# Weight sums of the MLP built from HBM to HBM during the mixers, and the first product's combinations on GpSimd

## The chip, the cores and the metric

The kernel runs on one core of one Trainium2 chip, in one launch. The metric is the device time of an execution in microseconds (us). In the profile PE is TensorE, PEld its weight loads, DVE is VectorE, ACT ScalarE, POOL GpSimd, and SP the engine that only issues DMAs.

## The reference

One decoder layer on 1024 tokens of width 1024, after 16 meta tokens, in fp32: an RMS norm and one input projection, three mixers (GLA, a gated linear attention with 4 heads; SWA, a sliding-window attention with 16 query heads; SSD, a Mamba-2 scan in 4 groups), their gated sum through an output projection, then the MLP that the change is about, and a last RMS norm.

```python
def _layer(x, ...):
    h = _rmsnorm(x, norm_mix)
    g_q, g_k, g_v, g_r, g_lr, s_q, s_k, s_v, m_z, m_xbc, m_dt, gate_logits = split(h @ w_in)
    y_a = _gla(...) @ w_branch_gla
    y_b = _swa(...) @ w_branch_swa
    y_c = _ssd(...) @ w_branch_ssd
    merged = gates[:, :, 0] * y_a + gates[:, :, 1] * y_b + gates[:, :, 2] * y_c
    x = x + (merged @ w_out) * vmask
    h2 = _rmsnorm(x, norm_mlp)
    x = x + (square(relu(h2 @ w_mlp_in)) @ w_mlp_out) * vmask     # 1024 -> 4096 -> 1024
    return x                                                       # then a last _rmsnorm
```

## The kernel before

**Products.** Every fp32 operand of a product is split into a rounded part (`hi`, type fp32r) and the rest (`lo`), and a product is three matmuls: hi times hi, hi times lo, lo times hi. ACT casts the `hi`, DVE subtracts for the `lo`. Weights come from HBM in tiles `w_raw` of 128x1024 (three buffers), whose halves go to `w_hi` and `w_lo`.

**Stages in their order:** norm and transposes (0 to 90 us), GLA (to 550), SWA (to 860), SSD (to 1580), the three branch products with their gates (to 1950), the output projection (to 2041), a transition in which the normed tokens `h2` are transposed and their combinations are formed and split (2041 to 2083), the first MLP product (to 2387), the second (2377 to 2737) and the last norm, written out at 2747.

**GLA** handles a head in 8 pairs of chunks. Each pair ends with a root on GpSimd (`rstd_of`, L88, named `grs`), DVE's scaling `og` and, after every fourth pair, transposes on TensorE. **SWA** has 32 blocks, in each of which GpSimd scales the weights `pe` (L540). **SSD** has 4 groups of 8 chunks. A chunk loads `ab` (512 KB, the sums of one group broadcast to all partitions, two buffers, L642), DVE and ACT make the decay matrix from it, TensorE multiplies it (L654), and GpSimd computes `y` (L662), `xe` (L669), the state `S` (L673) and the root `yrs` (L88).

**The MLP** is computed by Strassen-Winograd: both factors are taken as 2x2 blocks, and 7 products of blocks take the place of 8. The weight sums are s1 = a21+a22, s2 = s1+a11, s3 = a11+a21, s4 = s2+a12.
- The *first product* has 16 units of 256 columns (`w_unit`, `unit_a` to `unit_e`). Per unit: two loads of 512 KB, four sums on DVE (L922 to L925), seven splits (L933, L934), seven products of 12 matmuls with 512 columns. The outputs x11, x21, x22 of 128x512 and the negatives n12, n21 (ACT, L953) go to HBM. Only `unit_a` and `unit_b` of unit 0 (the products x11*a11 and x21*a12) stand in the transition.
- The *second product* has 4 quarters `q` of seven products of 48 matmuls (L1148 to L1151). Its operands are made by chains (`Chain`): SP loads the first summand, and GpSimd issues DMAs that add the next onto the tile in SBUF (L1105, `accum_op=add`, 512 KB each, 64 in all). A chain's tile is cast by L1124 (from the first product's outputs) or L1137 (weights), added to and cast again.

**What sets the order:** the framework orders each engine's instructions and each queue's DMAs when the program is built; on the chip every engine works through its list in order, waiting where a semaphore says so. DMAs of SP and ACT go through hardware queues, those of GpSimd through a software queue.

Of the kernel before, what the change touches and what calls it, by code (L numbers as in the profile page):

```python
# [8 lines left out]
F32 = mybir.dt.float32  # L9
# [7 lines left out]
P = 128  # L17
# [27 lines left out]
def hybrid_layer_kernel(ctx, tc, x, meta_tokens, norm_mix, w_in, b_gate, gla_w_gate_up, gla_b_gate_up,  # L45
# [37 lines left out]

    def rstd_of(ss, n, name, rows=P, cols=1):
# [3 lines left out]
        nc.gpsimd.tensor_tensor(rs[:rows, :cols], ms[:rows, :cols], mhalf[:rows, :cols], ALU.pow)  # L88
        return rs[:rows, :cols]
# [12 lines left out]
    def vec(nm, i):  # L102
# [11 lines left out]
             for q in range(8) for n in ("x11", "x21", "x22", "n12", "n21")}  # L114
# [4 lines left out]
    def w_split(loads, cols, scales=None):  # L119
        hi = wp.tile([P, 2048], F32R, tag="whi", name="w_hi")  # L120
        lo = wp.tile([P, 2048], F32R, tag="wlo", name="w_lo")
        h = cols // 2
        for i in range(2):
            raw = raw_tile()
            loads(raw[:, :h], i)
            c = slice(i * h, (i + 1) * h)
            if scales is None:
                nc.scalar.copy(hi[:, c], raw[:, :h])  # L128
                nc.vector.tensor_tensor(lo[:, c], raw[:, :h], hi[:, c].bitcast(F32), sub)  # L129
                continue  # L130
            n = cols // len(scales)
            for k in range(h // n):
                sc, rc, c = scales[i * (h // n) + k], slice(k * n, (k + 1) * n), slice(i * h + k * n, i * h + (k + 1) * n)
                nc.scalar.activation(hi[:, c], raw[:, rc], AF.Copy, scale=sc)
                nc.vector.scalar_tensor_tensor(out=lo[:, c], in0=raw[:, rc], scalar=sc, in1=hi[:, c].bitcast(F32),
                                               op0=mult, op1=sub)
        return hi, lo

    def w_cols(view, ranges, scales=None):
        tot = sum(n for _, n in ranges)  # L140

        def loads(raw, i):
            rv = raw.rearrange("p (k c) -> p k c", k=KD // 2)
            o = 0
            for c, n in ranges:
                nc.sync.dma_start(rv[:, :, o:o + n], view[:, i * (KD // 2):(i + 1) * (KD // 2), c:c + n])
                o += n
        hi, lo = w_split(loads, KD * tot, scales)
        return (hi[:, :KD * tot].rearrange("p (k c) -> p k c", k=KD),
                lo[:, :KD * tot].rearrange("p (k c) -> p k c", k=KD))  # L150
# [16 lines left out]
    with p1:  # L167
# [118 lines left out]
        def gla():  # L286
# [15 lines left out]
            for h in range(4):  # L302
# [95 lines left out]
                for p in range(8):  # L398
# [23 lines left out]
                    rs = rstd_of(ss, 256, "grs")  # L422
                    nc.vector.scalar_tensor_tensor(out=og, in0=o, scalar=rs, in1=rt[p], op0=mult, op1=mult)
# [87 lines left out]
        def swa_block(sp, bk, sinks, m0, m1, kh, kl, vv, vvm, qq, h0, b):  # L511
# [28 lines left out]
            nc.gpsimd.tensor_tensor(pe[:, :, :nk], pe[:, :, :nk], up(zs, 2, [P, 4, nk]), mult)  # L540
# [17 lines left out]
        def ssd(g):  # L558
# [79 lines left out]
            with tc.high_priority(offset=HPE):  # L638
                for c in range(NT):
# [39 lines left out]
                    rs = rstd_of(ss, CH, "yrs")  # L679
                    nc.scalar.activation(y, y, AF.Copy, scale=rs)  # L680
# [6 lines left out]
        with tc.tile_pool(name="dtp", bufs=1, reuse_waits="tile") as dp, bank_pool("bdt") as bk:  # L687
# [6 lines left out]
            hi, lo = w_split(loads, KD * 64)  # L694
            w = (hi[:, :KD * 64].rearrange("p (k c) -> p k c", k=KD), lo[:, :KD * 64].rearrange("p (k c) -> p k c", k=KD))
# [73 lines left out]
    with ExitStack() as p2:  # L769
# [140 lines left out]

        def w_unit(u):
            raws = []
            for i in range(2):
                raw = raw_tile().rearrange("p (k c) -> p k c", k=4)
                nc.sync.dma_start(raw, wmi_v[:, 4 * i:4 * i + 4, u * 256:(u + 1) * 256])
                raws.append(raw)
            k4 = "p (k c) -> p k c"
            a11, a21 = raws[0][:, :, 0:P], raws[0][:, :, P:2 * P]
            a12, a22 = raws[1][:, :, 0:P], raws[1][:, :, P:2 * P]
            s1, s3 = (v.rearrange(k4, k=4) for v in m_tile())  # L920
            s2, s4 = (v.rearrange(k4, k=4) for v in m_tile())
# [5 lines left out]
            for names in (((1, a11), (6, s2), (5, s1), (2, a12)), ((7, s3), (4, a22), (3, s4))):  # L927
                hi = wp.tile([P, 2048], F32R, tag="whi", name="w_hi")
                lo = wp.tile([P, 2048], F32R, tag="wlo", name="w_lo")
                for i, (n, src) in enumerate(names):  # L930
                    h = hi[:, i * 512:(i + 1) * 512].rearrange(k4, k=4)
                    l = lo[:, i * 512:(i + 1) * 512].rearrange(k4, k=4)
                    nc.scalar.copy(h, src)  # L933
                    nc.vector.tensor_tensor(l, src, h.bitcast(F32), sub)  # L934
                    out[n] = (h, l)
# [15 lines left out]
        def neg(g):  # L951
            n = g_tile()
            nc.scalar.activation(n, g, AF.Copy, scale=-1.0)  # L953
            return n

# [277 lines left out]
```

## Time and profile before

| | us |
|---|---|
| three runs | 2742.92, 2743.89, 2758.51 (median 2743.89) |
| the profiled execution | 2748.39 |
| its span, first to last instruction | 2746.7 |
| PE busy | 2630.9 (96%) |
| DVE, ACT, POOL busy | 1419.9 (52%), 1117.5 (41%), 402.3 (15%) |
| mean granted clock of TensorE | 0.974 of full speed |
| DMA packets | 249681, 294.04 MB |

An engine's share is a mean over stages. The tables of stretches below give each engine's busy time in a stretch, so that the time in which PE was not busy can be seen stage by stage; "clock" is what was granted of full speed. A wait is put down to what came last.

### The profile page before, as it was taken

The numbers are of one execution on the slowest core, as the hardware profiler recorded it, in microseconds if no ns is written. First come the engines' busy times: TensorE is split into PE (matmuls) and PEld (weight loads), VectorE is DVE, ScalarE is ACT, GpSimd is POOL, SyncE is SP. The second block draws the span as 40 slices with busy tenths as digits, with TensorE's granted clock in tenths as the row PEclk, the third lists the DMA queues.
The fourth block names the chain that finished last, engine by engine and source line by source line (L and its number), as shares of the span: only waits on it lengthen the run. The fifth ranks groups of instructions, "written<-read, shape, count | busy, mean of one in ns | idle before, by whom it ended". The sixth has DMA issues, their size and how long they took to land. (4 is left out here: it accounts for less than half of the span.)

```text
span 2746.7 us, 36564 instructions
## 1 busy us (share of the span) xinstructions
PE 2630.9 (96%) x14373; PEld 2255.5 (82%) x14373; DVE 1419.9 (52%) x2567; ACT 1117.5 (41%) x1971; POOL 402.3 (15%) x358
## 2 busy tenths in 40 slices
PE   8999999999999999999999899999998999889998
PEld 7998988888888979789889688888986888767776
DVE  5333323256664674655646643444447565555557
ACT  6423433256664364353453343332244333333334
POOL 1000000012220130220311301222210000022223
PEclk9999999999999999989999999999998999989999
DMA  4211112212223152251342464422322333788884
GB/s 140 63 44 50 47 47 66 73 56 74 62 66 90 54 135 65 75 141 55 85 116 61 120 234 146 153 100 92 123 93 79 132 112 130 238 205 177 185 184 115
DMA packets 249681, 294.04 MB, mean 107 GB/s; under 512 B 15535, under 2 KB 177637, under 8 KB 249509
## 3 DMA queue, kind: packets, MB, share of 16 engines
q1 hardware_dynamic: 184836, 203.55, 24.8%
q0 software_dynamic: 17408, 33.56, 7.2%
q10 hardware_dynamic: 47264, 54.60, 5.6%
q8 instruction: 113, 1.85, 0.3%
q14 instruction: 60, 0.48, 0.1%
HBM read 224.41 MB, written 67.24 MB: 106 GB/s over the span
## 5 line engine op out<-in xcount | busy, mean ns | idle before, releaser
L159 PE MATMUL acc_ps<-hh,w_hi 128*128 128x512 f32 (+6 forms) x1320 | 474.8, 360 | 3.2 <-ACT rt L353 1.7
L160 PE MATMUL acc_ps<-hl,w_hi 128*128 128x512 f32 (+6 forms) x1320 | 473.4, 359 | 0.0
L161 PE MATMUL acc_ps<-hh,w_lo 128*128 128x512 f32 (+6 forms) x1320 | 470.3, 356 | 0.0
L187 PE MATMUL acc_ps<-w_hi,hh 128*128 128x256 f32 x1056 | 306.3, 290 | 5.3 <-ACT zst L200 4.7
L188 PE MATMUL acc_ps<-w_lo,hh 128*128 128x256 f32 x1056 | 304.8, 289 | 0.0
L189 PE MATMUL acc_ps<-w_hi,hl 128*128 128x256 f32 x1056 | 304.0, 289 | 0.0
L159 PEld LDWEIGHTS acc_ps<-hh,w_hi 128*128 128x128 f32 (+1 forms) x1320 | 248.0, 188 | 33.8 <-issue 3.8
L160 PEld LDWEIGHTS acc_ps<-hl,w_hi 128*128 128x128 f32 (+1 forms) x1320 | 248.0, 188 | 26.7 <-issue 2.6
L161 PEld LDWEIGHTS acc_ps<-hh,w_lo 128*128 128x128 f32 (+1 forms) x1320 | 248.2, 188 | 25.0 <-issue 1.0
L129 DVE TENSOR_TENSOR w_lo<-w_raw,w_hi 128x1024 fp32r<-128x1024 f32 (+1 forms) x124 | 159.7, 1315 | 145.3 <-ACT w_hi L128 144.0
L1148 PE MATMUL pp_ps<-w_hi,o 128*128 128x512 f32 x448 | 183.0, 410 | 28.4 <-ACT o L1124 18.2
L187 PEld LDWEIGHTS acc_ps<-w_hi,hh 128*128 128x128 f32 x1056 | 198.2, 188 | 13.6 <-ACT zst L200 5.4
L189 PEld LDWEIGHTS acc_ps<-w_hi,hl 128*128 128x128 f32 x1056 | 198.4, 188 | 9.7 <-issue 8.9
L188 PEld LDWEIGHTS acc_ps<-w_lo,hh 128*128 128x128 f32 x1056 | 198.7, 188 | 5.0 <-issue 4.1
L787 PE MATMUL pp_ps<-o,w_hi 128*128 128x512 f32 x512 | 201.4, 398 | 0.0
L790 PE MATMUL pp_ps<-o,w_hi 128*128 128x512 f32 x512 | 200.4, 392 | 0.0
L128 ACT CAST w_hi<-w_raw 128x1024 fp32r<-128x1024 f32 (+1 forms) x124 | 122.7, 1036 | 179.0 <-PE acc_ps L160 69.2
L942 PE MATMUL pp_ps<-o,w_hi 128*128 128x512 f32 x448 | 179.3, 402 | 9.5 <-ACT o L153 9.2
L1150 PE MATMUL pp_ps<-w_lo,o 128*128 128x512 f32 x448 | 182.6, 408 | 0.2
L944 PE MATMUL pp_ps<-o,w_hi 128*128 128x512 f32 x448 | 179.3, 400 | 2.4 <-DVE o L154 2.4
L945 PE MATMUL pp_ps<-o,w_lo 128*128 128x512 f32 x448 | 178.5, 399 | 0.0
L1151 PE MATMUL pp_ps<-w_hi,o 128*128 128x512 f32 x448 | 176.4, 399 | 0.0
(319 smaller groups left out, 4986.4 us busy)
## 6 DMA issues: line engine op xcount, KB each, us to landing
w_raw<-in_w_in_dram SPq DMA_DIRECT2D x80, 512.0 KB, 3.8
ab<-acs_d SPq DMA_DIRECT2D x32, 512.0 KB, 8.7
g<-gate SPq DMA_DIRECT2D x64, 256.0 KB, 4.4
w_raw<-in_w_mlp_in_dram SPq DMA_DIRECT2D x32, 512.0 KB, 3.9
gate<-gst ACTq DMA_DIRECT2D x48, 256.0 KB, 2.0
hid_x<-hid ACTq DMA_DIRECT2D x48, 256.0 KB, 3.1
o<-hid_n POOLq DMA_DIRECT2D x24, 512.0 KB, 7.9
o<-in_w_mlp_out_dram POOLq DMA_DIRECT2D x24, 512.0 KB, 7.6
```

The source lines that it names most:

```text
L159: nc.tensor.matmul(ps, lhsT=lh, rhs=rh, start=(i == 0), stop=False)
L160: nc.tensor.matmul(ps, lhsT=lh, rhs=rl, start=False, stop=False)
L161: nc.tensor.matmul(ps, lhsT=ll, rhs=rh, start=False, stop=(i == n - 1))
L187: nc.tensor.matmul(o, lhsT=h_h, rhs=whi[:, k, off:off + width], start=(k == 0), stop=False)
L188: nc.tensor.matmul(o, lhsT=h_h, rhs=wlo[:, k, off:off + width], start=False, stop=False)
L189: nc.tensor.matmul(o, lhsT=h_l, rhs=whi[:, k, off:off + width], start=False, stop=(k == KD - 1))
L787: nc.tensor.matmul(ps[b], lhsT=lh, rhs=xs[b][:, 0, :], start=(st and k == 0), stop=(sp_ and k == n - 1))
L790: nc.tensor.matmul(ps[b], lhsT=lh, rhs=xs[b][:, 1, :], start=False, stop=False)
L942: nc.tensor.matmul(ps, lhsT=h[:, kk, :], rhs=x[:, 0, :], start=(first and kk == 0), stop=False, skip_group_check=True)
L944: nc.tensor.matmul(ps, lhsT=h[:, kk, :], rhs=x[:, 1, :], start=False, stop=False, skip_group_check=True)
L1148: nc.tensor.matmul(ps[t], lhsT=xh[:, ts], rhs=wh, start=(first and kk == 0), stop=False, skip_group_check=True)
L1150: nc.tensor.matmul(ps[t], lhsT=xh[:, ts], rhs=wl, start=False, stop=False, skip_group_check=True)
```

## The change

1. **Weight sums.** Two sets of arrays in HBM, `ws1` (for `w_mlp_in`, stored by unit) and `ws2` (for `w_mlp_out`), take s1 to s4. 64 DMAs of 1 MB from HBM to HBM build them, all issued by GpSimd: plain copies, then accumulations (`accum_op=add`) onto them. `prep_next` issues one directly behind each `grs` of GLA (32: heads 0 and 1 plain, heads 2 and 3 accumulating), behind every second `pe` of SWA (16) and behind the `yrs` of every second chunk of SSD (16: groups 0 and 1 plain and contiguous, groups 2 and 3 accumulating). A plain or accumulating DMA for `ws1` has 2048 rows of 512 bytes, for `ws2` 512 rows of 2 KB; a copy from one array to another is contiguous.
2. **First product.** `w_unit` loads s1 to s4 from `ws1` and a11, a12, a22 from the weights (256 KB each); the four sums on DVE and the negations on ACT go. GpSimd computes four combinations of the outputs per unit, t1 to t4, and ACT issues their DMAs to HBM.
3. **Units ahead.** For units 0 to 5 the products x11*a11 and x21*a12 move into the transition (`pre`). Their p1 goes to HBM and is loaded again in `unit_a`, x11 in `unit_e2`.
4. **Smaller tiles.** `w_hi` and `w_lo` have four buffers of 1024 columns instead of two of 2048.
5. **Second product.** Every operand is one plain load: t1 to t4, x11, x21, x22, s1 to s4 and the blocks of the weights. `Chain` is gone.

```diff
+    def prep():
+        for step in (((0, "a21"), (2, "a11")), ((0, "+a22"), (2, "+a21")), ((1, 2),), ((1, "+a22"),), ((3, 1),), ((3, "+a12"),)):
+            for n, src in step:
+                for g in range(4):
+                    if isinstance(src, int):
+                        nc.gpsimd.dma_start(ws1[n][4 * g:4 * g + 4], ws1[src][4 * g:4 * g + 4])
+                        yield 1
+                        nc.gpsimd.dma_start(ws2[n][g], ws2[src][g])
+                        yield 1
+                        continue
+                    dst = (ws1[n][:, :, g, :], ws2[n][g].rearrange("(v p) d -> v p d", p=P))
+                    for d, o in zip(dst, sum_src(g, src.lstrip("+"))):
+                        if src[0] == "+":
+                            nc.gpsimd.dma_start(d, o, accum_op=add)
+                        else:
+                            nc.gpsimd.dma_start(d, o)
+                        yield 1
...
+    def prep_next():
+        with tc.issue_after(on_pool[0].ins):
+            next(prepper, 0)
...
                     rs = rstd_of(ss, 256, "grs")
+                    prep_next()
...
-            nc.gpsimd.tensor_tensor(pe[:, :, :nk], pe[:, :, :nk], up(zs, 2, [P, 4, nk]), mult)
+            on_pool[0] = nc.gpsimd.tensor_tensor(pe[:, :, :nk], pe[:, :, :nk], up(zs, 2, [P, 4, nk]), mult)
+            if b % 2:
+                prep_next()
...
                     rs = rstd_of(ss, CH, "yrs")
+                    if c % 2:
+                        prep_next()
...
-            nc.vector.tensor_tensor(s1, a21, a22, add)
-            nc.vector.tensor_tensor(s2, s1, a11, add)
-            nc.vector.tensor_tensor(s3, a11, a21, add)
-            nc.vector.tensor_tensor(s4, s2, a12, add)
...
+            for n in range(2):
+                nc.sync.dma_start(v12[:, n], ws1[n][u])
...
+            for v in range(2):
+                w = [[t[:, :, v * P:(v + 1) * P] for t in pair] for pair in ws_]
+                a = ps_tile()
+                prod(a, w[0], "x11", True, True)
+                p1 = g_tile()
+                nc.scalar.copy(p1, a)
+                nc.scalar.dma_start(p1_d[u + v], p1)
+                unit_b(u + v, {"a": a, "w": {2: w[1]}})
...
+            t1, t2, t3, t4 = st["u3"], st["p1"], st["x12"], st["u2"]
+            nc.gpsimd.tensor_tensor(t1, st["x11"], g, sub)
+            hid_out(u, "t1", t1)
+            nc.gpsimd.tensor_tensor(t2, st["x22"], t1, add)
+            hid_out(u, "t2", t2)
+            nc.gpsimd.tensor_tensor(t3, g, st["x22"], sub)
+            hid_out(u, "t3", t3)
+            nc.gpsimd.tensor_tensor(t4, st["x21"], t2, sub)
+            hid_out(u, "t4", t4)
...
         for kk in range(4):
+            if kk * 2 < NPRE:
+                pre(kk * 2)
...
         for u in range(NU):
+            unit_a(u, sts[u])
+            unit_c(u, sts[u])
             if u:
-                unit_a(u, sts[u])
                 unit_e(u - 1, sts[u - 1])
+            unit_c2(u, sts[u])
+            if u:
+                unit_e2(u - 1, sts[u - 1])
+            if u >= NPRE:
                 unit_b(u, sts[u])
-            unit_c(u, sts[u])
             unit_d(u, sts[u])
...
-            product(b, x_op(xb, "x22", "n12"), w_op(wa, "a21"), True, True, evict("c22", sub))
+            product(b, x_op(q, "t3"), w_op(q, "s3"), True, True, evict("c22", add))
```

How the instructions stand on two engines at the places that matter, row by row (the numbers in names tell buffers apart).

POOL in GLA, the first head. Before, the eight roots stand behind each other (four are shown):

```order
L375 COPY qx_1784<-qd_1731 128x8x64
L88 TENSOR_TENSOR grs_1825<-ms_1823,mhalf_77 128x1
L88 TENSOR_TENSOR grs_1845<-ms_1843,mhalf_77 128x1
L88 TENSOR_TENSOR grs_1865<-ms_1863,mhalf_77 128x1
L88 TENSOR_TENSOR grs_1885<-ms_1883,mhalf_77 128x1
```

Now a DMA stands behind each, alternately of 2048 and of 512 rows:

```order
L425 COPY qx_1838<-qd_1785 128x8x64
L90 TENSOR_TENSOR grs_1879<-ms_1877,mhalf_77 128x1
L145 DMA ws1_0_193<-in_w_mlp_in_dram 2048x1x128
L90 TENSOR_TENSOR grs_1900<-ms_1898,mhalf_77 128x1
L145 DMA ws2_0_0_197<-in_w_mlp_out_dram 512x1x512
L90 TENSOR_TENSOR grs_1921<-ms_1919,mhalf_77 128x1
L145 DMA ws1_0_193<-in_w_mlp_in_dram 2048x1x128
L90 TENSOR_TENSOR grs_1942<-ms_1940,mhalf_77 128x1
L145 DMA ws2_0_1_198<-in_w_mlp_out_dram 512x1x512
```

The roots keep their order; each but the first has a DMA issue ahead of it on POOL.

ACT in the first product, from unit 1 to unit 2 (`hid` are outputs, `mt` the tiles of t1 to t4, `ws` the loaded sums). Before, the casts of a unit stand among the outputs of the unit before:

```order
L933 CAST w_hi_18325<-w_raw_18315 128x512
L933 CAST w_hi_18325<-w_raw_18317 128x512
L933 CAST w_hi_18325<-mt_18319 128x512
L968 COPY mt_18356<-pp_ps_18343 128x512
L933 CAST w_hi_18325<-mt_18320 128x512
L949 DMA hid0_x22_133<-hid_18311 128x512
L949 DMA hid0_x21_132<-hid_18371 128x512
L953 ACTIVATE hid_18375<-hid_18371 128x512
L933 CAST w_hi_18335<-mt_18319 128x512
```

Now the casts of the next unit stand behind the four DMAs of t1 to t4, each of which waits for GpSimd:

```order
L1018 DMA hid0_x21_132<-hid_18674 128x512
L1018 DMA hid0_t1_134<-mt_18575 128x512
L1018 DMA hid0_t2_135<-mt_18574 128x512
L1018 DMA hid0_t3_136<-mt_18575 128x512
L1018 DMA hid0_t4_137<-mt_18574 128x512
L972 CAST w_hi_18740<-ws_18732 128x512
L1018 DMA hid0_x22_133<-hid_18728 128x512
L972 CAST w_hi_18740<-ws_18732 128x512
L972 CAST w_hi_18746<-w_raw_18736 128x512
```

Per unit ACT has five casts instead of seven in units 0 to 5, and the four DMAs of one unit stand ahead of the casts of the unit after next.

PE in the transition. Before, the last transposes of `h2` (L901) are followed at once by unit 0's products of the last combinations (L942 and on, `o` are the split tokens):

```order
L901 MATMUL pp_ps_18105<-ident_72,h2_17906 128x128
L901 MATMUL pp_ps_18105<-ident_72,h2_17915 128x128
L901 MATMUL pp_ps_18105<-ident_72,h2_17924 128x128
L901 MATMUL pp_ps_18105<-ident_72,h2_17933 128x128
L942 MATMUL pp_ps_18130<-o_18021,w_hi_17952 128x512
L942 MATMUL pp_ps_18144<-o_18024,w_hi_17952 128x512
```

Now matmuls of the moved products (L1011 to L1014) stand between the transposes (L955):

```order
L1013 MATMUL pp_ps_18454<-o_18140,w_hi_18411 128x512
L1014 MATMUL pp_ps_18454<-o_18140,w_lo_18412 128x512
L955 MATMUL pp_ps_18519<-ident_72,h2_18152 128x128
L1011 MATMUL pp_ps_18234<-o_18092,w_hi_18198 128x512
L1013 MATMUL pp_ps_18234<-o_18092,w_hi_18198 128x512
L1014 MATMUL pp_ps_18234<-o_18092,w_lo_18199 128x512
L1011 MATMUL pp_ps_18234<-o_18111,w_hi_18198 128x512
L1013 MATMUL pp_ps_18234<-o_18111,w_hi_18198 128x512
```

In all 144 matmuls of the moved products stand in this stretch, where 24 stood.

## Rows read from the trace of the kernel before

**Rows 1.** The page's first part: busy time of PE, share of the span, instructions.

```profile
PE 2630.9 (96%) x14373; PEld 2255.5 (82%) x14373; DVE 1419.9 (52%) x2567; ACT 1117.5 (41%) x1971; POOL 402.3 (15%) x358
```

**Rows 2.** Stretches of the program; columns in the first row, numbers of instructions in brackets.

```profile
core 0: us, PE busy (x) PEld busy (x) DVE busy (x) ACT busy (x) POOL busy (x), PEclk, DMA share, GB/s
95.00:550.00 455.00, 452.77 (x2919) 405.15 (x2918) 136.28 (x263) 152.99 (x282) 24.98 (x42) 1.00 0.17 52
...
955.00:1036.00 81.00, 72.32 (x473) 60.62 (x471) 55.70 (x126) 48.36 (x67) 23.32 (x25) 0.92 0.49 128
...
2041.00:2083.00 42.00, 27.72 (x94) 17.84 (x93) 36.28 (x62) 30.85 (x57) 5.06 (x4) 0.76 0.11 32
...
2060.00:2070.00 10.00, 4.77 (x9) 2.60 (x10) 10.00 (x18) 6.62 (x12) 0.00 (x0) 0.69 0.07 26
...
2083.00:2387.00 304.00, 304.00 (x1307) 244.90 (x1306) 187.27 (x292) 108.25 (x182) 4.98 (x4) 1.00 0.42 136
2377.00:2390.00 13.00, 13.00 (x58) 10.42 (x57) 6.64 (x9) 1.05 (x1) 2.40 (x2) 1.00 1.07 311
2390.00:2440.00 50.00, 31.80 (x105) 24.37 (x104) 15.79 (x15) 13.99 (x17) 10.88 (x9) 0.76 0.92 244
...
2500.00:2510.00 10.00, 5.53 (x15) 4.08 (x14) 3.56 (x4) 2.25 (x3) 2.44 (x2) 0.71 0.54 96
2510.00:2737.00 227.00, 221.02 (x934) 176.27 (x934) 149.92 (x183) 86.77 (x109) 59.06 (x51) 0.99 0.75 162
```

**Rows 3.** Waits from 2377 to 2740 us (PE, ACT) and from 940 to 1600 (DVE).

```profile
engine line waited for: us in total, times, longest us
PE pp_ps L1148 <- ACT o L1124: 18.2, 3, 8.5
...
ACT o L1124 <- DMA o<-hid_n: 80.6, 14, 11.5
...
DVE ab L646 <- DMA ab<-acs_d: 81.6, 26, 6.2
```

**Rows 4.** The page's DMA issues: count, KB each, us from issue to landing.

```profile
ab<-acs_d SPq DMA_DIRECT2D x32, 512.0 KB, 8.7
```

**Rows 5.** Groups of instructions: line, engine, operation, count | busy us, mean ns of one.

```profile
L128 ACT CAST w_hi<-w_raw 128x1024 fp32r<-128x1024 f32 (+1 forms) x124 | 122.7, 1036 | 179.0 <-PE acc_ps L160 69.2
...
L129 DVE TENSOR_TENSOR w_lo<-w_raw,w_hi 128x1024 fp32r<-128x1024 f32 (+1 forms) x124 | 159.7, 1315 | 145.3 <-ACT w_hi L128 144.0
...
L933 ACT CAST w_hi<-mt 128x512 fp32r<-128x512 f32 x60 | 37.2, 620 | 57.8 <-DVE mt L922 49.2 <-PE pp_ps L944 6.9
...
L934 DVE TENSOR_TENSOR w_lo<-mt,w_hi 128x512 fp32r<-128x512 f32 x60 | 41.2, 687 | 0.9 <-ACT w_hi L933 0.9
...
L826 POOL TENSOR_TENSOR mg<-mg,g 128x512 f32<-128x512 f32 x48 | 71.6, 1524 | 296.3 <-DVE g L825 296.3
...
L673 POOL TENSOR_TENSOR S<-S,decb 128x512 f32<-128x512 f32 x28 | 38.9, 1388 | 13.6 <-DVE S L674 13.1
```

**Rows 6.** One line's instructions: DMA issues of ACT and POOL, ns min/median/max.

```profile
L949 ACTq DMA_DIRECT2D hid_x<-hid x48: 326/326/342, 2061.6 to 2392.4; - x48
...
L1105 POOL DMA_DIRECT2D o<-hid_n x24: 1197/1203/1712, 2364.5 to 2678.6; - x24
```

**Rows 7.** The page's DMA queues: packets, MB, share of 16 engines over the span.

```profile
q1 hardware_dynamic: 184836, 203.55, 24.8%
q0 software_dynamic: 17408, 33.56, 7.2%
```

**Rows 8.** POOL in order of time in GLA: start, us, [idle before <- releaser].

```profile
274.80 0.55 POOL L88 TENSOR_TENSOR grs<-ms,mhalf 128x1 f32<-128x1 f32 x1 [4.01 <-DVE ms L86]
279.36 0.55 POOL L88 TENSOR_TENSOR grs<-ms,mhalf 128x1 f32<-128x1 f32 x1 [4.01 <-DVE ms L86]
```

**Rows 9.** The same view in a chunk loop of SSD.

```profile
1343.73 0.55 POOL L88 TENSOR_TENSOR yrs<-ms,mhalf 128x1 f32<-128x1 f32 x1 [5.48 <-DVE ms L86]
1344.32 1.44 POOL L673 TENSOR_TENSOR S<-S,decb 128x512 f32<-128x512 f32 x1
1347.94 1.04 POOL L662 TENSOR_TENSOR y<-xT,db 128x512 f32<-128x512 f32 x1 [2.19 <-PE ps_tr L632]
```

More of the change, by code (lines that the diff above doesn't have):

```diff
@@ L113, in hybrid_layer_kernel @@
     hid_d = {(q, n): dram.tile([256, 512], F32, name=f"hid{q}_{n}")
-             for q in range(8) for n in ("x11", "x21", "x22", "n12", "n21")}
+             for q in range(8) for n in ("x11", "x21", "x22", "t1", "t2", "t3", "t4")}
+    NPRE = 6
+    p1_d = [dram.tile([P, 512], F32, name=f"p1d{i}") for i in range(NPRE)]
+    ws1 = [dram.tile([16, P, 4, P], F32, name=f"ws1_{n}") for n in range(4)]
+    ws2 = [[dram.tile([512, 512], F32, name=f"ws2_{n}_{g}") for g in range(4)] for n in range(4)]
@@ L116, in raw_tile, with __init__, __getitem__ @@
+    prepper = prep()
+    def prep_next():
+        with tc.issue_after(on_pool[0].ins):
+            next(prepper, 0)
     def raw_tile():
         return wp.tile([P, 1024], F32, tag="raw", name="w_raw", bufs=RB)
[L119 to L122, printed above, removed]
+    class WT:
+        def __init__(self, tiles, width):
+            self.per = len(tiles) and KD // len(tiles)
+            self.tiles = [t[:, :self.per * width].rearrange("p (k c) -> p k c", k=self.per) for t in tiles]
+        def __getitem__(self, idx):
+            p_, k, c = idx
+            return self.tiles[k // self.per][p_, k % self.per, c]
@@ L123, in w_split, with hilo @@
+    def hilo():
+        return (wp.tile([P, 1024], F32R, tag="whi", name="w_hi", bufs=4),
+                wp.tile([P, 1024], F32R, tag="wlo", name="w_lo", bufs=4))
+    def w_split(loads, width, scales=None):
+        his, los = [], []
+        h = KD // 2 * width
         for i in range(2):
+            hi, lo = hilo()
+            his.append(hi)
+            los.append(lo)
             raw = raw_tile()
             loads(raw[:, :h], i)
-            c = slice(i * h, (i + 1) * h)
             if scales is None:
-                nc.scalar.copy(hi[:, c], raw[:, :h])
-                nc.vector.tensor_tensor(lo[:, c], raw[:, :h], hi[:, c].bitcast(F32), sub)
+                nc.scalar.copy(hi[:, :h], raw[:, :h])
+                nc.vector.tensor_tensor(lo[:, :h], raw[:, :h], hi[:, :h].bitcast(F32), sub)
@@ L130, in w_split @@
                 continue
[L131 to L135, printed above, removed]
+            for k in range(KD // 2):
+                sc, c = scales[i * (KD // 2) + k], slice(k * width, (k + 1) * width)
+                nc.scalar.activation(hi[:, c], raw[:, c], AF.Copy, scale=sc)
+                nc.vector.scalar_tensor_tensor(out=lo[:, c], in0=raw[:, c], scalar=sc, in1=hi[:, c].bitcast(F32),
@@ new lines, in hybrid_layer_kernel, with w_pair @@
+        k4 = "p (k c) -> p k c"
+        def w_pair(srcs):
+            hi, lo = hilo()
+            out = []
+            for i, src in enumerate(srcs):
+                h, l = (t[:, i * 512:(i + 1) * 512].rearrange(k4, k=4) for t in (hi, lo))
+                nc.scalar.copy(h, src)
+                nc.vector.tensor_tensor(l, src, h.bitcast(F32), sub)
+                out.append((h, l))
+            return out
+        def w_unit(u):
+            s12, s34 = (mp.tile([P, 1024], F32, tag="m", name="ws") for _ in range(2))
+            v12, v34 = (t.rearrange("p (n k c) -> p n k c", n=2, k=4) for t in (s12, s34))
+            pre_u = u < NPRE
+            for n in range(2):
+                nc.sync.dma_start(v12[:, n], ws1[n][u])
+            raw = raw_tile()
+            a12, a22 = (raw[:, i * 512:(i + 1) * 512].rearrange(k4, k=4) for i in range(2))
+            c0 = u * 256
+            out = {}
+            if pre_u:
+                nc.sync.dma_start(a22, wmi_v[:, 4:8, c0 + P:c0 + 2 * P])
+            else:
+                raw1 = raw_tile()
+                a11 = raw1[:, 0:512].rearrange(k4, k=4)
+                nc.sync.dma_start(a11, wmi_v[:, 0:4, c0:c0 + P])
+                nc.sync.dma_start(a12, wmi_v[:, 4:8, c0:c0 + P])
+                nc.sync.dma_start(a22, wmi_v[:, 4:8, c0 + P:c0 + 2 * P])
+            for n in range(2):
+                nc.sync.dma_start(v34[:, n], ws1[n + 2][u])
+            s1, s2, s3, s4 = v12[:, 0], v12[:, 1], v34[:, 0], v34[:, 1]
+            if pre_u:
+                out[6], out[5] = w_pair((s2, s1))
+            else:
+                out[1], out[6] = w_pair((a11, s2))
+                out[5], out[2] = w_pair((s1, a12))
+            out[7], out[4] = w_pair((s3, a22))
+            out[3], = w_pair((s4,))
@@ L976, in unit_b @@
             hid_out(u, "x11", g)
+            st["x11"] = g
         def unit_c(u, st):
```

149 lines of the change are left out of this document (65 added, 84 removed).

## The prediction

> **What bounds the kernel now.** I read the page first, then the stages one after another. TensorE is busy 2630.9 us of a span of 2746.7 [rows 1], and the change leaves the number of matmuls as it is: 1 344 in each of the two MLP products and all others. So it can gain only where TensorE stands still or is slowed, and lose wherever it makes TensorE wait anew. The table of stages [rows 2] shows where that is. In the first product, 2083 to 2387, PE is busy 304.00 us of 304 with 1307 matmuls, 0.2326 us each: nothing to gain there. Three other places have room. (a) The transition, 2041 to 2083: 42 us with 94 instructions, PE 27.72 us busy, clock 0.76, while DVE is busy 36.28 and, from 2060 to 2070, all 10.00 us. (b) The second product: 2390 to 2440 has 105 matmuls, worth 24.4 us, in 50; 2500 to 2510 has 15, worth 3.5, in 10; 2510 to 2737 has 934, worth 217.2, in 227. The waits name the place: PE's L1148 waits for the casts L1124 (18.2 us in three waits), and these casts wait for the tiles that the accumulating DMAs fill (80.6 us for o<-hid_n alone) [rows 3]. (c) The chunk loops of SSD, of which one is shown, 955 to 1036: PE 72.32 of 81 us, DMA share 0.49 [rows 2]. There DVE waits 81.6 us in 26 of 32 chunks for the load of ab, 512 KB that land after 8.7 us [rows 3, 4]. The change reduces (a) and (b) and puts new traffic on (c) and on GLA (95 to 550: PE 452.77 of 455, nothing to gain).
>
> The sum is made against the profiled execution, 2748.4 us, which is 4.5 above the median of 2743.9.
>
> **Transition: -22 us.** Two products of six blocks, 144 matmuls, stand there instead of those of one block, 24: 120 x 0.2326 = 27.9 us leave the full stretch of the first product. They count in so far as the transition doesn't grow. If all its 94 instructions cost as much as a matmul of 512 columns (21.9 us), PE alone would need 21.9 + 27.9 = 49.8 us, 7.8 more than now; but most are transposes of 128 columns, so that this is an upper bound. DVE gets six splits of 128x1024, 6 x 1.32 = 7.9, and loses block 0's four additions and seven splits, 11 x 0.69 = 7.6 [rows 5]: no change. ACT gets 6 casts x 1.04, 6 times a copy, a Relu and a Square (about 0.6 each, 10.9 by the cast's 0.62) and 12 DMA issues x 0.33, 21 in all, and loses seven casts x 0.62 = 4.3 and some 2 of block 0 [rows 5, 6]: 31 + 15 = 46 us. So it grows by 2 to 8 us by PE and by 4 by ACT. I take 6: 28 - 6 = 22. Ends: 26 and 10 (the moved work waits for its own splits).
>
> **Second product: -39 us.** 64 accumulating DMAs go, and with them the chains load, accumulate, cast. The losses of (b) are 25.6 + 6.5 + 9.8 = 42. What is left must be fed by plain loads: 2 MB per product of 48 matmuls, 11.2 us, that is 188 GB/s, plus 4 MB of x2b at the start. From 2377 to 2390 the queues moved 311 GB/s [rows 2], enough for both, and six of x2b's eight loads stand behind those of the first two products. I leave 3 us for the start. Ends: 42, and 25 (only the first hole closes).
>
> **First product: +8 us.** GpSimd gets four additions per block, 4 x 1.39 to 1.52 = 5.8 us [rows 5], in blocks of 60 matmuls (14.0 us, six blocks) or 84 (19.5). ACT waits for them in its order: behind the last product of a block come two DVE operations (1.4), GpSimd (5.8) and the issue, 7.5 us in all, and only then the casts of the block after next, 0.62 and 0.69 for the split. That is 8.8 of 14.0: hidden, and the four additions and one negation that left make DVE and ACT lighter. What may show is the loop through p1: in the six short blocks its tile comes free only when the results written from it have left, and the reload follows. I saw no wait of PE in this stretch before, so 0 is the lower end; six blocks x 5 us, were GpSimd's whole chain to come late, is the upper, 30. I take 8, nearer the row.
>
> **SSD: +22 us.** Sixteen copies or accumulations of 1 MB come behind the yrs of the odd chunks. Plain traffic of the hardware queue cost 24.8% of 2746.7 us for 203.55 MB, 3.35 us of all 16 engines per MB; accumulating, 7.2% for 33.56 MB, 5.9 [rows 7]. Were each to delay a load of ab by its whole length: 8 x 3.35 + 8 x 5.9 = 74 us, the upper end; zero is the lower. Between two users I give each half: 37; three of four odd chunks of a group have a chunk behind them, and 26 of 32 chunks waited for ab: 37 x 0.75 x 0.81 = 22. By the Trainium skill, DMA: Bandwidth & Descriptors, Queues, rings and completion order, each DMA engine goes round its queues packet by packet, which speaks against the change here; no trace so far has both kinds of traffic over an ab load.
>
> **GLA and SWA: 0.** Each grs stands 4.0 us behind the end of the one before [rows 8]; an issue between them that lasts 1.2 us, as those of 256 rows do [rows 6], fits in. The DMAs themselves run beside a PE that waits for no load. What if the cover goes is the first rival. The smaller w_hi and w_lo tiles hold as much as before: 0.
>
> Sum: -22 - 39 + 8 + 22 = -31, so 2717 for such an execution and **2713** beside the median.
>
> **Rivals.** *GpSimd's issue grows with rows* (the other side). Ends: 1.2 us whatever the rows, or in proportion, 8 x 1.2 = 9.6 for 2048 rows and 2.4 for 512. It decides from 4.0 us on, the room between two grs. At 9.6 a pair of grs with its two DMAs takes 9.6 + 2.4 + 1.1 = 13.1 us where 9.1 is the pace; three such pairs of a head (the fourth has the pause behind it), four heads: 48 us in front of TensorE's transposes. In SSD four such DMAs stand right in front of S, which follows yrs without a gap [rows 9]: 4 x (9.6 - 2.2, the gap behind) = 30. So -31 + 78 = +47: 2791. For it: every issue known here has 256 rows, and nothing shows a larger one. Against it: nothing but that the 64 issues seen are all close to 1.20, whatever they move. By the Trainium skill, the same page, Anatomy of one DMA, many descriptors can be emitted before the cost shows, which gives my sum; by its section SWDGE vs HWDGE vs iDMA, software computes a pair of descriptors per piece, which gives this rival. No run here has tried more than 256 rows. Chance 0.20.
>
> *The ab loads lose more, or the first product does*: SSD at 50 instead of 22 gives 2741; the first product at 30 instead of 8 gives 2735. For it: the chunk loops have no slack at all; four of the accumulations come in 2048 pieces of 512 bytes, where those priced here had 272 packets each [rows 7]. Against: half of the sixteen are contiguous copies. Within 1%: chance 0.25.
>
> *The gains come whole and the loads share well*: -26 - 42 + 0 + 5 gives 2681. For it: the losses are all bounds without a row of their own. Chance 0.15.
>
> **How the numbers follow.** My forecast has the chance 0.40. About 1% (27 us, to 2716.5) is what a measurement can tell from no change. The forecast lies just below it: three quarters of its chance (0.31) fall under the line, and the third rival adds 0.15: faster 0.46. The rest of the forecast and most of the second rival: same 0.31. The first rival and a little of the second: slower 0.23. The range runs from the full gains, 2748 - 68 - 4.5 = 2676, less some for a shorter start, to a GpSimd issue of some 9 us: 2670 to 2785. That leaves out perhaps 0.04 below and 0.14 above.
>
> **What would show it.** Transition: 144 matmuls of 512 columns there at a clock near 1, the stretch under 50 us. Second product: no wait of its matmuls longer than 2 us after the first 10 us. SSD: the waits of DVE's ab grow from 82 to about 105 us. GLA: the issues of L145 with 2048 rows last as long as those with 512. I am wrong if these issues last over 4 us, if PE waits in the first product by more than 30 us, or if the ab loads of a chunk with a DMA behind yrs land as late as the DMA.

## The result, and the profile after

The changed kernel takes **2788.9 us** in the median (2786.3 to 2792.5, 4 runs) where the kernel before takes 2747.5 beside it (2742.9 to 2758.5, 4 runs): ratio 1.0146, interval 1.011 to 1.0181. It is slower by 1.5%, outside the range of 2670 to 2785, and on the other side of the forecast of 2713. The profiled execution took 2792.5 us.

The MLP became faster, as forecast, and the mixers slower by nearly twice as much. One row per stage shows it: a line's matmuls with the start of the first and of the last (count, ns min/median/max, us). Before: GLA's last transposes (L429), SSD's products with ab (L654), the two MLP products.

```profile
L429 PE MATMUL ps_tr<-ident,og x64: 270/272/273, 180.6 to 523.0; 128*128 128x128 f32 x64
...
L654 PE MATMUL ps_y<-xd,ab x512: 217/275/474, 955.7 to 1578.0; 128*128 128x64 f32 x171
...
L942 PE MATMUL pp_ps<-o,w_hi x448: 389/392/796, 2041.0 to 2387.6; 128*128 128x512 f32 x150
...
L1148 PE MATMUL pp_ps<-w_hi,o x448: 390/393/792, 2376.9 to 2737.4; 128*128 128x512 f32 x150
```

The same lines of the changed kernel:

```profile
L480 PE MATMUL ps_tr<-ident,og x64: 270/272/476, 179.4 to 539.4; 128*128 128x128 f32 x64
...
L707 PE MATMUL ps_y<-xd,ab x512: 217/275/473, 978.5 to 1654.8; 128*128 128x64 f32 x171
...
L1011 PE MATMUL pp_ps<-o,w_hi x448: 387/393/504, 2136.7 to 2470.7; 128*128 128x512 f32 x150
...
L1237 PE MATMUL pp_ps<-w_hi,o x448: 390/393/628, 2460.4 to 2781.6; 128*128 128x512 f32 x150
```

Read as a ledger: GLA ends 16 us later, SSD's first product 23 later, its last 77, and the transition begins 96 later (2136.7 against 2041.0). From there 13 us come back up to the end of the first product (346.6 us became 334.0) and 39 up to the end of the second (349.8 became 310.9). 96 - 13 - 39 = 44, the whole loss.

The stretches that answer to [rows 2], of the changed kernel (PE, PEld, DVE, ACT, POOL busy, clock, DMA share, GB/s): GLA, SSD's first and last chunk loop, the start of the branch products, the transition, the two products.

```profile
95.00:560.00 465.00, 448.70 (x2865) 400.96 (x2865) 134.83 (x261) 153.66 (x279) 73.94 (x74) 0.98 0.54 122
978.00:1060.00 82.00, 70.24 (x444) 59.04 (x443) 56.02 (x116) 44.20 (x61) 25.85 (x27) 0.90 0.63 156
1566.00:1655.00 89.00, 71.56 (x307) 53.32 (x306) 51.31 (x104) 23.74 (x40) 30.22 (x25) 0.84 0.59 121
1668.00:1690.00 22.00, 10.67 (x45) 8.37 (x45) 2.52 (x3) 2.85 (x6) 0.00 (x0) 0.86 0.74 222
2137.00:2190.00 53.00, 48.59 (x220) 37.78 (x219) 39.53 (x65) 40.67 (x75) 3.02 (x4) 1.00 0.42 140
2190.00:2470.00 280.00, 275.21 (x1176) 219.93 (x1175) 148.63 (x220) 76.95 (x130) 81.81 (x60) 1.00 0.63 209
2470.00:2782.00 312.00, 310.01 (x1327) 250.70 (x1326) 213.45 (x249) 121.83 (x146) 17.78 (x16) 0.99 0.58 196
```

The page's busy times and queues, which answer to [rows 1] and [rows 7] (packets, MB, share of 16 engines):

```profile
PE 2637.8 (95%) x14373; PEld 2265.1 (81%) x14373; DVE 1392.8 (50%) x2497; ACT 1094.3 (39%) x1928; POOL 484.6 (17%) x422
...
q1 hardware_dynamic: 219460, 248.65, 29.9%
q0 software_dynamic: 77056, 67.36, 12.5%
```

PE has the same work as before in a longer span; the software queue has four times the packets. In the transition PE is now busy 48.59 of 53 us at a granted clock of 1.00, and in the second product 310.01 of 312: both holes are closed. GLA, where PE had 452.77 of 455, now misses 16 of 465, and at 1668 PE stands half idle. Before, the 22 us that lie as far behind SSD's last ab product were full:

```profile
1591.00:1613.00 22.00, 22.00 (x96) 17.72 (x95) 8.86 (x14) 11.94 (x21) 0.00 (x0) 1.00 0.98 360
```

The new DMAs themselves: issue on POOL (ns min/median/max), first the plain ones of GLA (L145), then the accumulating ones (L143).

```profile
L145 POOL DMA_DIRECT2D ws<-in_w_mlp_in_dram x8: 1076/1076/1252, 175.7 to 296.6; - x8
L145 POOL DMA_DIRECT2D ws<-in_w_mlp_out_dram x8: 1158/1158/1167, 180.3 to 301.2; - x8
...
DMA to landing us min/median/max: 6.8/15.3/17.3
...
L143 POOL DMA_DIRECT2D ws<-in_w_mlp_in_dram x16: 1831/1865/1919, 362.5 to 1648.7; - x16
L143 POOL DMA_DIRECT2D ws<-in_w_mlp_out_dram x16: 1902/1944/1962, 367.2 to 1661.2; - x16
...
DMA to landing us min/median/max: 11.1/29.6/36.9
```

2048 rows take no longer to issue than 512 (1.08 and 1.16 us), so the first rival's mechanism is not there, though its 2791 us is near the time. An accumulating DMA lands after 30 us in the median, up to 37; which form takes how long stands under e3. And in GLA an issue is held (POOL in order of time: start, us, idle before):

```profile
376.30 1.96 POOL L143 DMA_DIRECT2D ws<-in_w_mlp_out_dram  x1
380.20 0.56 POOL L90 TENSOR_TENSOR grs<-ms,mhalf 128x1 f32<-128x1 f32 x1 [1.94 <-DVE ms L88]
395.30 1.88 POOL L143 DMA_DIRECT2D ws<-in_w_mlp_in_dram  x1 [14.54 <-issue]
396.40 1.36 POOL L90 TENSOR_TENSOR grs<-ms,mhalf 128x1 f32<-128x1 f32 x1
```

The fifth accumulation of the head starts 14.5 us after the root ahead of it; the next root, ready long before, stands behind it. The first accumulation had landed by then (at 373.6); the second, issued at 367.19, landed after 27.8 us, and the held issue starts 0.3 us later. So three were under way while it was held. DVE's `og` waits 12.7 us for that root, and TensorE for `og`. PE's waits from 170 to 560 us (us in total, times, longest):

```profile
PE ps_tr L480 <- DVE og L474: 14.4, 2, 9.7
```

In SSD, just ahead of it and behind it the loads are late. DVE's wait for ab, 860 to 1700 us, answers to the last row of [rows 3] (which has 81.6 us from 940 on, 95.2 in these limits):

```profile
DVE ab L699 <- DMA ab<-acs_d: 149.5, 30, 22.3
```

and at the start of the branches ACT waits for the first operands (1655 to 1720 us):

```profile
ACT o L203 <- DMA o_raw<-ogla: 25.3, 5, 18.7
```

while the last accumulation, issued at 1661, is still moving: o_raw landed after 8.5 us before, now after 21.8.

```profile
o_raw<-ogla SPq DMA_DIRECT2D x6, 512.0 KB, 21.8
...
ws<-in_w_mlp_out_dram POOLq DMA_DIRECT2D x1, 1024.0 KB, 36.9
```

### The profile page after: what moved, and what is told of

It is laid out like the page before. It is cut to its first block, busy times and chain, and to the rows that moved or that the text cites. A ratio compares the mean times of both kernels' runs of the same rounds, so it can differ in the third digit from the quotient of the medians.

```text
span 2790.8 us, 36978 instructions
## 1 busy us (share of the span) xinstructions
PE 2637.8 (95%) x14373; PEld 2265.1 (81%) x14373; DVE 1392.8 (50%) x2497; ACT 1094.3 (39%) x1928; POOL 484.6 (17%) x422
## 3 DMA queue, kind: packets, MB, share of 16 engines
q0 software_dynamic: 77056, 67.36, 12.5%
## 4 chain that ended last, share of the span: by engine, by line
PE 78%; DMA 11%; DVE 4%; ACT 3%; issue 2%; SPq 1%; POOL 0%; ACTq 0%; DVEq 0%; POOLq 0%
DMA ab<-acs_d 8%; PE pp_ps L841 8%; PE acc_ps L209 8%; PE acc_ps L210 8%; PE acc_ps L211 8%; PE pp_ps L844 4%; PE pp_ps L1011 4%; PE pp_ps L1013 4%; PE pp_ps L1014 4%; PE pp_ps L1239 4%; PE pp_ps L1240 4%; PE pp_ps L1237 4%; PE acc_ps L237 3%; PE acc_ps L239 3%; PE acc_ps L238 3%
## 5 line engine op out<-in xcount | busy, mean ns | idle before, releaser
L209 PEld LDWEIGHTS acc_ps<-hh,w_hi 128*128 128x128 f32 (+1 forms) x1320 | 249.2, 189 | 45.1 <-ACT gst L261 10.6
L841 PE MATMUL pp_ps<-o,w_hi 128*128 128x512 f32 x512 | 202.6, 400 | 12.7 <-ACT o L203 11.7
L181 ACT CAST w_hi<-w_raw 128x1024 fp32r<-128x1024 f32 (+1 forms) x124 | 128.3, 1036 | 194.9 <-PE acc_ps L210 81.4
L1011 PE MATMUL pp_ps<-o,w_hi 128*128 128x512 f32 x448 | 177.2, 398 | 7.8 <-DVE mt L1078 3.9
L1240 PE MATMUL pp_ps<-w_hi,o 128*128 128x512 f32 x448 | 177.1, 396 | 0.0
L1237 PE MATMUL pp_ps<-w_hi,o 128*128 128x512 f32 x448 | 174.2, 395 | 1.3 <-ACT w_hi L1226 1.3
L1014 PE MATMUL pp_ps<-o,w_lo 128*128 128x512 f32 x448 | 172.7, 395 | 0.0
```

Source lines behind the costliest of these rows:

```text
L209: nc.tensor.matmul(ps, lhsT=lh, rhs=rh, start=(i == 0), stop=False)
L841: nc.tensor.matmul(ps[b], lhsT=lh, rhs=xs[b][:, 0, :], start=(st and k == 0), stop=(sp_ and k == n - 1))
L1011: nc.tensor.matmul(ps, lhsT=h[:, kk, :], rhs=x[:, 0, :], start=(first and kk == 0), stop=False, skip_group_check=True)
L1240: nc.tensor.matmul(ps[t], lhsT=xl[:, ts], rhs=wh, start=False, stop=(last and kk == 3), skip_group_check=True)
```

## The experiments

All are edits of the changed kernel, each timed beside the kernel before on its chip (ratio, with its 95% interval). The runs are from several chips, so that small differences between two of them are better read from the ratios than from the times.

**Without the DMAs (e1).**

```diff
     def prep_next():
         with tc.issue_after(on_pool[0].ins):
-            next(prepper, 0)
+            pass
...
```

The MLP loads other arrays of the same shapes. Expected:

> Leaves out the 64 DMAs that build the weight sums; the MLP loads blocks of the weights of the same size in their place, so its output is not the reference's. All theories but one put the loss on these DMAs: GLA to the branch products then take what they took before, and the two MLP products keep their 52 us of gain: about 2696 us. If the smaller tiles or the new order cost time ahead of the MLP, it stays above 2730.

Measured: 2698.3 us, ratio 0.9824 (0.9803 to 0.9846). The 64 DMAs cost 90.6 us (88 by the ratios), and everything else in the change is worth 48. The last ab product of SSD starts at 1576.6, as before (1578.0), so the smaller tiles and the new order cost nothing in sum ahead of the MLP. SSD by itself isn't as before, though: it takes 631.5 us from its first to its last ab product, where the kernel before took 622.3, while GLA ends 5 us earlier and SWA is 5 shorter. In e4, e6, e7 and e8, which have no DMA in SSD either, it takes 637.1, 635.9, 641.3 and 640.3: so 631.5 to 641.3 is what SSD takes without them, and a price in SSD is not known to better than these 10 us. DVE's wait for ab falls back to 87 us:

```profile
L707 PE MATMUL ps_y<-xd,ab x512: 217/275/473, 945.1 to 1576.6; 128*128 128x64 f32 x171
...
DVE ab L699 <- DMA ab<-acs_d: 87.2, 27, 6.3
```

**Plain copies only (e2).**

```diff
-                            nc.gpsimd.dma_start(d, o, accum_op=add)
+                            nc.gpsimd.dma_start(d, o)
```

> All 32 accumulating DMAs become plain copies of the same rows at the same places (the sums are not formed). Theory A, accumulating DMAs cost because each keeps the DMA engines busy for long: the roots of GLA heads 2 and 3 no longer stand behind a held issue, SSD's groups 2 and 3 lose as little as groups 0 and 1, about 2712 us. Theory B, any DMA issued in GpSimd's line costs, whatever it does: 2780 or more.

Measured: 2737.6 us, ratio 0.9967 (0.9955 to 0.9979): between both theories. GLA loses nothing now, with all 32 DMAs in it (the last transpose starts at 517.9 us, e1: 517.8). SSD still takes 662.7 us from the first to the last ab product, where it takes 631.5 to 641.3 without DMAs and 676.3 in the changed kernel; DVE's wait for ab is 125.8 us. So accumulating costs much, but a plain copy over an ab load is not free either.

```profile
L707 PE MATMUL ps_y<-xd,ab x512: 217/275/476, 948.6 to 1611.3; 128*128 128x64 f32 x171
```

**Contiguous accumulations (e3).**

```diff
...
-                            nc.gpsimd.dma_start(d, o, accum_op=add)
+                            m_ = 0 if n else 2
+                            if i == 0:
+                                nc.gpsimd.dma_start(ws1[n][4 * g:4 * g + 4], ws1[m_][4 * g:4 * g + 4], accum_op=add, max_dma_last_dim=8192)
+                            else:
+                                nc.gpsimd.dma_start(ws2[n][g], ws2[m_][g], accum_op=add, max_dma_last_dim=8192)
```

> The 32 accumulating DMAs stay at their places and add as many bytes, but from one contiguous array onto another in pieces of 8 KB (other sums than the reference's). If the cost of an accumulating DMA is in its 512 or 2048 small pieces: landing in under 10 us and about 2712 us. If it is in accumulating as such (reading the target, adding): landings near 30 us and 2780 or more.

Measured: 2724.9 us, ratio 0.9926 (0.9903 to 0.9948). The same adding lands after 10 us, not 30, and its issue takes 0.85 us, so the cost is mostly in the form of the DMA, not in adding as such:

```profile
L145 POOL DMA_DIRECT2D ws<-ws x16: 813/844/948, 361.0 to 1594.6; - x16
...
DMA to landing us min/median/max: 7.9/10.1/15.4
```

It missed 2712 by 13 us. SSD keeps 654.4 us, 13 to 23 above the kernels without DMAs there: sixteen DMAs of 1 MB over the ab loads cost about 1 us each even in the best form.

What in the form costs is not settled. Two accumulations of the changed kernel in SWA, each issued with nothing else on the queue, one in 512-byte pieces (at 738.6), one in pieces of 2 KB (at 754.0):

```profile
ws<-in_w_mlp_in_dram POOLq DMA_DIRECT2D x1, 1024.0 KB, 11.3
...
ws<-in_w_mlp_out_dram POOLq DMA_DIRECT2D x1, 1024.0 KB, 30.3
```

So the smaller pieces land earlier, and small size alone is not what takes 30 us. In the packet records of these traces an accumulation in pieces of 2 KB mostly has three or four packets under way at a time (1467.7 to 1497.8, where it is alone), one in 512-byte pieces (738.6 to 749.9) and those of 8 KB in e3 mostly 14 or more. The view of `ws2` has an outermost dimension of 4, that of `ws1` one of 16, and a contiguous array is cut in 128 pieces: a spread over few DMA engines would fit, and e3 changed this together with the pieces. No run separates the two.

**The same DMAs at other places (e4).**

```diff
-                    prep_next()
+                    if h < 2 or p % 2:
+                        prep_next()
...
-                    if c % 2:
-                        prep_next()
...
-                            nc.gpsimd.tensor_tensor(m, m, g, add)
+                            on_pool[0] = nc.gpsimd.tensor_tensor(m, m, g, add)
+                            slot[0] += 1
+                            if slot[0] % 3 == 0:
+                                prep_next(2 if 4 < (slot[0] - 15) // 3 <= 8 else 1)
```

> The same 64 DMAs, sums as the reference's, at other places: GLA heads 2 and 3 take one behind every second root, SWA 20, SSD none, and the last 20 stand behind GpSimd's additions in the branch products, where TensorE waited for nothing. Theory A (what costs is where an accumulation meets a tight load or a root): 2700 to 2715 us. If the traffic costs its engine time wherever it stands: 2780 or more.

Measured: 2743.2 us, ratio 0.9985 (0.9972 to 0.9998). The place is worth 46 us: GLA ends at 520.0, SSD takes 637.1. But the expectation of 2700 to 2715 was too low: from SSD's last ab product to the first MLP product 491.1 us pass (e1: 465.4). The branch products, which had no wait before, pay 26 us for 20 DMAs, 12 of them accumulations, and SWA, which has 12 accumulations instead of 8, takes 438.3 us (e1: 427.3).

**ACT's queue instead of GpSimd's (e5),** as e2 but SSD's sixteen from ACT:

```diff
-                    if c % 2:
-                        prep_next()
-                    nc.scalar.activation(y, y, AF.Copy, scale=rs)
+                    yc = nc.scalar.activation(y, y, AF.Copy, scale=rs)
+                    if c % 2:
+                        act[0] = True      # prep() then issues on nc.scalar
+                        on_pool[0] = yc
+                        prep_next()
```

> As the kernel with plain copies only, but the sixteen DMAs of SSD are issued by ACT, behind its scaling by yrs, instead of GpSimd (the sums are not formed). Theory T, their traffic delays the loads of ab: SSD, first to last product with ab, stays near 660 us, the whole near 2737. Theory G, the issue in GpSimd's line (1.1 us ahead of S) delays the chain of states: near 635 us and 2712.

Measured: 2737.6 us, as e2; SSD takes 662.5 us, e2 662.7. Theory G falls: in SSD the traffic of plain copies costs, not their issue in GpSimd's line.

**GLA's accumulations in fours (e9).**

```diff
...
-                    prep_next()
+                    if h < 2 or p == 7:
+                        prep_next(1 if h < 2 else 4)
...
-                nc.gpsimd.tensor_copy(qx[:, :, 0, :], qdr[:, :, 0, :])
+                on_pool[0] = nc.gpsimd.tensor_copy(qx[:, :, 0, :], qdr[:, :, 0, :])
+                if h >= 2:
+                    prep_next(4)
```

> The changed kernel with the sixteen accumulations of GLA heads 2 and 3 in fours: four behind the copy qx of a head, four behind its last root, so that no root stands behind a fifth. All else as changed. Theory H, GpSimd's issue is held while four are under way and the roots behind it come late: the last transposes of GLA end near 520 us instead of 539, the whole 15 to 20 us below the changed kernel, about 2770. Theory T, their traffic keeps GLA's loads waiting: GLA ends near 539 and the whole stays near 2789.

Measured: 2775.8 us, ratio 1.0095 (1.0068 to 1.0122), 13 us below the changed kernel by the medians and 20 between the profiled executions (2772.2 and 2792.5); GLA's last transpose starts at 519.5 us, and PE no longer waits for og there. Same DMAs, same stage, so theory H holds in GLA: the price was the root behind a held issue. One detail was not expected: the fourth of a burst is held too, by 6.7 us. It starts 0.3 us after the first of the burst has landed (12.1 us after its issue at 394.25), so that three under way are enough, not four:

```profile
L484 PE MATMUL ps_tr<-ident,og x64: 270/272/273, 179.2 to 519.5; 128*128 128x128 f32 x64
...
394.25 1.88 POOL L143 DMA_DIRECT2D ws<-in_w_mlp_in_dram  x1
395.33 2.75 POOL L143 DMA_DIRECT2D ws<-in_w_mlp_out_dram  x1
396.42 3.52 POOL L143 DMA_DIRECT2D ws<-in_w_mlp_in_dram  x1
406.64 1.91 POOL L143 DMA_DIRECT2D ws<-in_w_mlp_out_dram  x1 [6.70 <-issue]
```

**Without SSD's eight accumulations (e10).**

```diff
-        for step in (..., ((3, 1),), ((3, "+a12"),)):
+        for step in (..., ((3, 1),)):
```

> The changed kernel without the last eight accumulations (s4 lacks a12), those of SSD's groups 2 and 3; the eight contiguous copies of groups 0 and 1 stay. If these eight carry SSD's loss and the late start of the branches: SSD's third and fourth chunk loop take 67 to 74 us instead of 81 and 88, the whole is 45 to 55 us below the changed kernel, about 2738. If the loss is spread over all sixteen DMAs of SSD: 2760 or more.

Measured: 2739.3 us, ratio 0.9962 (0.995 to 0.9975): these eight cost 49.7 us, over 6 each. The third and fourth loop last 68.8 and 73.9 us (changed: 81.3 and 88.2; first to last ab product), and the way from SSD to the transition is back at 465.6 (481.9). All of SSD takes 643.7 us with the eight copies:

```profile
L707 PE MATMUL ps_y<-xd,ab x512: 217/275/476, 976.0 to 1619.7; 128*128 128x64 f32 x171
```

**A version that uses this (e6).** All copies in small pieces stand in GLA, where e2 had 32 for nothing; all adding is contiguous and stands in SWA, behind every pe.

```diff
+        for n, o in ((0, "a21"), (2, "a11"), (1, "a22"), (3, "a12")):
+            for g in range(4):
+                dst = (ws1[n][:, :, g, :], ws2[n][g].rearrange("(v p) d -> v p d", p=P))
+                for d, s in zip(dst, sum_src(g, o)):
+                    nc.gpsimd.dma_start(d, s)
+                    yield 1
+        for n, m in ((2, 0), (0, 1), (1, 2), (3, 1)):
+            for g in range(4):
+                nc.gpsimd.dma_start(ws1[n][4 * g:4 * g + 4], ws1[m][4 * g:4 * g + 4], accum_op=add, max_dma_last_dim=8192)
+                yield 1
+                nc.gpsimd.dma_start(ws2[n][g], ws2[m][g], accum_op=add, max_dma_last_dim=8192)
+                yield 1
...
-            if b % 2:
-                prep_next()
+            prep_next()
...
-                    if c % 2:
-                        prep_next()
```

> Sums as the reference's, other DMAs: all 32 copies in small pieces stand in GLA, behind every root, where plain copies cost nothing; the 32 accumulations add one contiguous array onto another in pieces of 8 KB (s3 = a11 + a21, s1 = a21 + a22, s2 = a22 + s3, s4 = a12 + s2), one behind every pe of SWA; SSD and the branches have none. If the cost is where small pieces and accumulations meet tight loads: 2700 to 2710 us. If SWA can't take 32 accumulations 8 us apart, each landing after some 10: held issues, pe late, 2725 or more.

Measured: **2706.6 us**, ratio 0.9841 (0.9827 to 0.9856), 8 above e1, which has no such DMAs, and 5 by the ratios, whose intervals overlap: it beats the kernel before by 1.6% and the changed one by 82 us. Sixty-four DMAs of 1 MB still move, with 10.6% of the DMA engines' time against 12.5%, but GLA is full again and SSD's last loop is as before (the last row is the kernel before's):

```profile
95.00:560.00 465.00, 463.14 (x2970) 414.47 (x2969) 144.14 (x274) 160.11 (x292) 60.81 (x74) 1.00 0.39 125
...
1507.00:1582.00 75.00, 66.77 (x306) 49.46 (x306) 48.74 (x104) 23.01 (x37) 26.08 (x22) 0.91 0.52 113
...
1505.00:1580.00 75.00, 65.90 (x311) 49.62 (x309) 49.79 (x105) 24.72 (x41) 25.98 (x24) 0.91 0.41 113
```

**The units moved ahead, none and eight (e7, e8),** as e6 with `NPRE = 0` and `NPRE = 8`.

> As e6_best, but no products moved into the transition, no reload of p1 and x11. By the prediction's steps the move is worth 14 us net (22 in the transition less 8 in the first product): 14 to 25 us above e6_best. If the rest of the change already filled the transition, or its DVE and ACT work only shift: within 5 us of it.

Measured: 2718.7 us, 12.1 above e6 on the same chip: the move is worth 12, where the prediction's steps had 14; just under the 14 to 25 expected.

> As e6_best with eight units moved ahead instead of six. If the transition still waits for TensorE's operands (DVE, ACT) and has room for matmuls: 4 to 9 us below e6_best. If six fill it: the same, within 3 us, or above, since two more units reload p1 and x11.

Measured: 2705.7 us, the same as e6: two units more bring nothing.

## Why the prediction was wrong, point by point

**Transition and first product, -22 + 8 = -14: right in the sum.** The stretch from the first to the last matmul of the first product became 12.6 us shorter, and e7 prices the move at 12.1. The transition takes 53 us for 220 instructions at a clock of 1.00 (I had said under 50), 11 more than before where I took 6, ACT being busy 40.67 us of it, where I had reckoned 46. From 2190 to 2470 PE is not busy for 4.8 us, where I took 8: the two errors offset each other. GpSimd is busy 81.81 us there; ACT's casts wait for it twice, 18.9 us together, but no wait of PE is over 1.7.

**Second product, -39: right.** 349.8 us became 310.9. The longest wait of PE in it is 1.3 us.

**GLA and SWA, 0: wrong, the first failed step.** I let an issue "that lasts 1.2 us" fit between two roots and said that the DMAs run beside a PE that waits for no load. I priced the issue alone, and not what stands behind an issue that can't start. In GLA accumulations land after 24 us (512-byte pieces) or 30 (2 KB), one is offered every 4.6 to 6.6 us, and when three are under way the next issue is held, with the root behind it. e9 shows it: 13 to 20 us come back by keeping roots out from behind held issues. A row that could have warned was at hand: in the second product of the kernel before, accumulations of 0.5 MB in pieces of 2 KB (L1105) took 7.5 us to land, so that twice the bytes would not be done in the 4 us between two roots:

```profile
DMA to landing us min/median/max: 5.6/7.5/15.0
```

From GLA's last transposes to SSD's first ab product the changed kernel takes 439.1 us and e1 427.3. SWA's blocks keep their pace up to the 29th of 32 (292.2 us behind GLA's last transposes in the changed kernel and in e3); the 12 us are lost from there on, where the last accumulations in SWA's order are moving (the very last issued at 858.9, landed after 33.4 us). SSD's first two ab loads land after 21.5 us there, where e3, whose accumulations are contiguous, has 8.8 and takes 427.6 us over the stretch (850 to 895 us, changed kernel and e3):

```profile
ab<-acs_d SPq DMA_DIRECT2D x2, 512.0 KB, 21.5
...
ab<-acs_d SPq DMA_DIRECT2D x2, 512.0 KB, 8.8
```

So this is SSD's mechanism, at a place where the sum had nothing.

**SSD, +22: the term mis-sized.** Its place and mechanism were right: traffic over the ab loads, not GpSimd (e5, for plain copies). The measured price is 35 to 45 us in SSD (676.3 against 631.5 to 641.3 without DMAs) and 16 more that the last accumulations carry into the branches (481.9 against 465.4), together 51 to 61. The engine time per MB was not far off: with plain copies the software queue used 7.4% of 2736.8 us for 67.26 MB, 3.0 us per MB (I had 3.35), and in the changed kernel 12.5% of 2790.8; the 146 us more, spread over 32 accumulations, make 3.0 + 4.6 = 7.6 us each (I had 5.9). What failed was the reasoning behind: half for sharing, times 0.75, times 0.81. By these prices, estimated as means over the whole queue, the sixteen use 8 x 3.0 + 8 x 7.6 = 85 us of all engines, and 51 to 61 us, 60 to 72%, came through to the end. DVE's wait for ab grew by 54 us (149.5 against 95.2), where I had said 23 (82 to 105). I also forgot who is late next behind the last group: the operands of the branches.

**The rivals.** The first gave 2791 and the sign, but that its time came so near is luck: its mechanism is not there, 2048 rows are issued in 1.08 us. It was right only in that roots come late behind an issue, which is held and not long. By the Trainium skill, DMA: Bandwidth & Descriptors, Anatomy of one DMA, many descriptors can be emitted before the cost shows; the trace agrees for plain copies, where four times the rows take no longer. The second, ab loads losing more, was the right one, and my end for it, 50 us, was too low, while 74 would have held. By the Trainium skill, DMA: Bandwidth & Descriptors, Queues, rings and completion order, the DMA engines go round their queues packet by packet; that the ab loads are late whichever queue issues (e2, e5) fits this, and no run here shows the order of packets.

**Ledger of the loss,** 90.6 us by e1: the held roots of GLA 13 to 20 (e9), SSD's eight accumulations 50 with the branches (e10), SSD's eight copies 2 to 12 (e10's SSD takes 643.7 us, the kernels without DMAs there 631.5 to 641.3: not clear of their spread), the way from SWA to SSD some 12. That is 77 to 94.

## What to carry to other kernels

Background DMAs are not free because a queue is idle: price the time on the DMA engines by the form of the DMAs (copying or adding, pieces, spread) from a row of the same form, and put them where nothing waits for a load, or for the engine that issues them. The same 64 MB cost 91, 45 and 5 to 8 us here (changed kernel, e4, e6 against e1), by place and form alone. Build sums from contiguous arrays: copy in small pieces once, plainly, and let the accumulations run in large pieces.

## What the runs showed that was not expected

- An accumulating DMA of 1 MB from HBM to HBM that finds GpSimd's queue empty lands after 11.3 us in pieces of 512 bytes and after 30.3 in pieces of 2 KB (L143); in GLA, behind others, the first form takes 24.3 us in the median. In pieces of 8 KB it takes about 10 us (e3; e6: 9.0 to 9.7). A plain copy in the small pieces takes 15 us (L145), a contiguous one 5.8.
- GpSimd's issue of an accumulating DMA takes 1.87 to 1.94 us in small pieces, 0.85 in pieces of 8 KB; a plain one 1.08 to 1.16, a contiguous copy 0.57. The number of rows, 512 or 2048, hardly matters.
- The issue of an accumulation in small pieces is held while three earlier ones have not landed, and starts 0.3 us after one of them lands: so in all eight cases of the changed kernel's GLA and all four of e9, with idle times of up to 14.5 us. A fourth plain copy is not held: at 203.24, in GLA's first head, one of 2048 rows goes out at once behind three with 3072 rows that have not landed. So neither the number of DMAs nor that of rows is the limit by itself. An accumulation in small pieces is 2064 packets, a plain copy 272 or 1040 (together with 32 for each contiguous copy they make the queue's 77056), so that a limit in packets would fit; no run tried it.
